# Gate and up of a decoder block in written order on all engines: three tiles ahead, staged work put on streams, reloads tied to progress, the up-side norm factor applied in the end

## The chip, the cores and the metric

The kernel runs on one core of a Trainium2 chip. The metric is the device time in microseconds (us) of one execution: the median of several runs of one program, where lower is better. Beside it stands one execution taken by the hardware profiler, which records every instruction of the engines: TensorE (PE, with its weight loads PEld), VectorE (DVE), ScalarE (ACT), GpSimd (POOL), and SyncE (SP), which only issues transfers. ScalarE and POOL issue transfers too.

## The reference

A decoder block of 256 tokens (16 meta tokens in front), width 2048: a projection into RWKV-7 time mixing and a forgetting attention, gated merge, output projection, then the feed-forward part. The change touches what stands behind the merge:

```python
merged = g_a * (y_a @ w_a) + g_b * (y_b @ w_b)
h = h + merged @ w_o                                          # (256, 2048)
gate, up = jnp.split(_rms(h, n2) @ w_gu, 2, axis=-1)          # w_gu: 2048 x 11264
return h + (jax.nn.silu(gate) * up) @ w_dn                    # w_dn: 5632 x 2048
```

`_rms` divides each token by the root of its mean square (the norm factor, one number per token) and multiplies by `n2`. Everything is float32. The matrix products run in fp32r on operands split into a high and a low part (`split`: ScalarE writes the high part as a copy in fp32r, VectorE the rest as a difference), as three products: high by high, low by high, high by low.

## The kernel before, in words

**Weights.** A weight tile is 128 partitions x 1024 elements, 0.5 MB. SP loads it into `raw`, ScalarE writes `wh` (L340), VectorE `wl` (L341), and TensorE multiplies by it. A job is a pair of functions, `load` and `mul`; `run` calls the load of one job before the `mul` of the job ahead of it. Outside the stages named below, a scheduler puts the instructions of each engine in an order by its own costs.

**Output projection.** Its tiles add to `hh` (the residual `h`, tokens on partitions), which is turned by TensorE, multiplied by `n2`, split into `hts` (features on partitions: the input of gate and up, not yet divided by the norm factor) and combined into sums of tokens, `hs0` to `hs7` (`sums_of_tokens`): each is split and written to DRAM by POOL (L1334).

**Gate and up.** The 5632 columns of each of gate and up are 11 groups of 512. Groups 0 to 7 (`PLAIN`) are multiplied plainly: eight tiles of gate, then eight of up per group (`gt`, `up`), the result with features on partitions, in four PSUM banks, the "main" ones. `halves` brings a bank to SBUF in two steps, a copy by ScalarE (L452) and an add by VectorE (L453). The gate's result is multiplied by the norm factor per token (`rsb`) and goes through Silu; the up's is multiplied by `rsb` (L1458) and by the gate (L1459), and split into `ach` and `acl`, the input of the down projection. For the groups of 256 features in `FAST`, sums of tokens `ss<i>` are built as above in one buffer (tag `hb`, `bufs=1`) and written to DRAM.

Groups 8 to 10 (`BLOCK`) are multiplied in 2 x 2 blocks with seven products in place of eight (a Strassen-Winograd scheme), in the four other, "aux", banks (`bg`, `bh`). A block tile `fr` has two halves: `load0` splits three of its four blocks into `fh` and `fl` (L515, L516) and forms four differences in place (L1492), `mul0` does three products; `load1` splits the differences into `wh`, `wl`, `mul1` does four products. The sums of tokens `hs` are the other operand: POOL reloads them from DRAM into `home` tiles (L1437). After the last tile of a block group, ScalarE and VectorE add the seven products up (`sums`, L1539), VectorE multiplies by the norm factor and by the gate (L1552), and a stream (`spawn`, called later by the planned clock that `slot` advances) turns the result by TensorE and splits it.

`todo` mixes the jobs: the block groups start at the places `STARTS`, and there one plain tile follows each half of a block tile. Only TensorE keeps the written order (`manual_schedule`); the order on the other engines is the scheduler's.

**Down projection.** Groups in `FAST` use the block scheme (`fast_jobs`: weights `q`, sums `sst` reloaded by POOL, products `dnp`), the others plain tiles (`slow_jobs`, products `dn`); both add to the main banks, and at the end of each half of the columns the banks are added to `hh`, reloaded from DRAM by POOL. All reloads of a half are issued ahead of its first tile (`sums_of`: L1598 for `sst`, L1600 for the fourth sum, which goes over an `ach` and `acl` block no longer needed).

## Time and profile before

| | |
|---|---|
| median of 3 runs | 1528.63 us (1527.79 to 1531.24) |
| profiled execution | 1529.84 us, its span 1528.1 us |
| granted TensorE clock, mean | 0.996 of full speed |
| TensorE busy | 1504.0 us of the span (98%) |
| weight loads, VectorE, ScalarE, POOL busy | 1343.3, 1241.2, 834.0, 134.9 us |
| moved | 306 MB, 201 GB/s over the span |

The span is the profiled execution from its first to its last record; its own time is 1.7 us longer. Gate and up take from about 788 to 1287 us, the down projection from there to the end. A row of instructions shows line, engine, operation, out<-in and shape, xcount, then busy time, mean duration in ns, and the idle time ahead of them with what ended most of it.

### The profile page before, as it was taken

Reading aid. Unit: us, or ns where it says so; the run is one execution under the profiler, and the core shown is the slowest. Engines: PE = TensorE matmul, PEld = TensorE weight load, DVE = VectorE, ACT = ScalarE, POOL = GpSimd, SP = SyncE. Lnnn points to the kernel's source line nnn. Section 1 sums busy time; section 2 is a strip of 40 time slices with the busy share of each in tenths; the row PEclk is TensorE's granted clock in tenths of the full one; section 3 lists DMA queues with packets and bytes.
Section 4 is the critical chain, followed back from the end, with each engine's and each line's share of the span. In section 5 each row is a group of like instructions: output and inputs, shape, how many; then the busy total and the mean of one; then the engine's idle time right before and its main releaser. Section 6 shows DMA issues by size and latency. Waiting matters only on the chain.

```text
span 1528.1 us, 26980 instructions
## 1 busy us (share of the span) xinstructions
PE 1504.0 (98%) x10320; PEld 1343.3 (88%) x10320; DVE 1241.2 (81%) x2180; ACT 834.0 (55%) x1212; POOL 134.9 (9%) x239
## 2 busy tenths in 40 slices
PE   9999999999999999999998999999999999899999
PEld 9999999999989888998887998998989888788887
DVE  7888699689789758776685888888898887698987
ACT  7754665465475546554454555555545555455553
POOL 2112202302202100000010000000000000200000
PEclk9999999999999999999999999999999999999999
DMA  8557356545645757767787666466775767966662
GB/s 270 166 173 203 116 157 196 168 125 169 186 125 161 222 139 231 237 215 252 255 276 240 195 214 200 148 198 218 216 224 182 223 184 209 377 224 205 223 214 84
DMA packets 217714, 306.45 MB, mean 201 GB/s; under 512 B 25136, under 2 KB 135232, under 8 KB 217456
## 3 DMA queue, kind: packets, MB, share of 16 engines
q1 hardware_dynamic: 202048, 277.25, 59.0%
q0 software_dynamic: 9488, 20.98, 4.0%
q10 hardware_dynamic: 6048, 6.49, 1.2%
q8 instruction: 81, 1.33, 0.4%
q14 instruction: 49, 0.40, 0.1%
HBM read 285.90 MB, written 18.78 MB: 199 GB/s over the span
## 4 chain that ended last, share of the span: by engine, by line
PE 83%; DVE 10%; issue 3%; DMA 2%; ACT 2%; SPq 0%; POOL 0%; DVEq 0%; ACTq 0%; POOLq 0%
PE zg L446 8%; PE up L446 5%; PE gt L446 5%; PE zg L448 4%; PE dn L1616 4%; PE dn L1614 4%; PE dn L1615 3%; DVE wl L341 3%; PE up L448 2%; PE gt L448 2%; PE f L446 2%; PE br L370 2%; PE br L371 2%; PE br L372 2%; PE f L370 2%
## 5 line engine op out<-in xcount | busy, mean ns | idle before, releaser
L341 DVE TENSOR_TENSOR wl<-raw,wh 128x1024 fp32r<-128x1024 f32 x402 | 489.7, 1225 | 112.3 <-ACT wh L340 110.2
L340 ACT ACTIVATE wh<-raw 128x1024 fp32r<-128x1024 f32 x402 | 421.7, 1055 | 256.7 <-PE br L371 40.6
L446 PE MATMUL gt<-hts,wh 128*128 128x512 f32 x512 | 181.0, 396 | 1.8 <-DVE ub L453 1.8
L446 PE MATMUL up<-hts,wh 128*128 128x512 f32 x512 | 180.0, 394 | 1.8 <-DVE gates L453 1.7
L446 PE MATMUL zg<-xhl,wh 128*128 128x512 f32 x512 | 181.2, 399 | 0.0
L448 PE MATMUL gt<-hts,wl 128*128 128x256 f32 x480 | 134.8, 281 | 0.0
L448 PE MATMUL up<-hts,wl 128*128 128x256 f32 x480 | 134.4, 280 | 0.0
L448 PE MATMUL zg<-xhl,wl 128*128 128x256 f32 x480 | 134.3, 280 | 0.0
L515 ACT ACTIVATE wh<-fr 128x1024 fp32r<-128x1024 f32 x48 | 50.9, 1061 | 115.6 <-DVE fr L1492 112.4
L446 PEld LDWEIGHTS gt<-hts,wh 128*128 128x128 f32 x512 | 95.0, 189 | 20.2 <-DVE ub L453 3.2
L446 PEld LDWEIGHTS up<-hts,wh 128*128 128x128 f32 x512 | 94.5, 188 | 19.8 <-DVE gates L453 2.7
L446 PEld LDWEIGHTS zg<-xhl,wh 128*128 128x128 f32 x512 | 94.3, 188 | 18.8 <-issue 0.7
L1614 PE MATMUL dn<-wh,ach 128*128 128x512 f32 x257 | 101.3, 394 | 1.0 <-ACT wh L515 1.0
L1615 PE MATMUL dn<-wh,acl 128*128 128x512 f32 x257 | 100.7, 392 | 0.0
L1616 PE MATMUL dn<-wl,ach 128*128 128x512 f32 x257 | 100.3, 394 | 0.1
L516 DVE TENSOR_TENSOR wl<-fr,wh 128x1024 fp32r<-128x1024 f32 x48 | 58.8, 1225 | 46.5 <-ACT wh L515 45.1
L448 PEld LDWEIGHTS gt<-hts,wl 128*128 128x128 f32 x480 | 91.2, 190 | 1.1
L448 PEld LDWEIGHTS zg<-xhl,wl 128*128 128x128 f32 x480 | 90.9, 189 | 1.2
L448 PEld LDWEIGHTS up<-hts,wl 128*128 128x128 f32 x480 | 90.9, 189 | 1.0
L1492 DVE TENSOR_TENSOR fr<-fr 128x256 f32<-128x256 f32 x192 | 80.9, 421 | 3.9
L515 ACT ACTIVATE wh<-tt 128x1024 fp32r<-128x1024 f32 x38 | 40.4, 1062 | 67.6 <-PE dn L1615 58.7
L370 PE MATMUL f<-xhl,wh 128*128 128x272 f32 x256 | 75.9, 296 | 0.0
(756 smaller groups left out, 3926.6 us busy)
## 6 DMA issues: line engine op xcount, KB each, us to landing
raw<-in_w_in_dram SPq DMA_DIRECT2D x160, 512.0 KB, 3.8
raw<-in_w_gate_up_dram SPq DMA_DIRECT2D x128, 512.0 KB, 4.5
raw<-in_w_down_dram SPq DMA_DIRECT2D x50, 512.0 KB, 4.7
fr<-in_w_gate_up_dram SPq DMA_DIRECT2D x48, 512.0 KB, 3.7
q<-in_w_down_dram SPq DMA_DIRECT2D x38, 512.0 KB, 5.8
raw<-in_w_o_dram SPq DMA_DIRECT2D x32, 512.0 KB, 5.0
raw<-in_w_branch_a_dram SPq DMA_DIRECT2D x16, 512.0 KB, 4.6
raw<-in_w_branch_b_dram SPq DMA_DIRECT2D x16, 512.0 KB, 4.0
```

Source lines behind the costliest of these rows:

```text
L340: nc.scalar.activation(th, rr, AF.Copy)
L341: nc.vector.tensor_tensor(tl, rr, th.bitcast(F32), op=ALU.subtract)
L370: nc.tensor.matmul(ps, wh, ah, start=first, stop=False)
L371: nc.tensor.matmul(ps, wh, al, start=False, stop=False)
L446: nc.tensor.matmul(ps.rearrange("p (a t) -> p a t", a=2), wh, act, start=first, stop=last)
L448: nc.tensor.matmul(ps[:, :T], wl, act[:, 0, :], start=False, stop=False)
L515: nc.scalar.activation(hi, src, AF.Copy)
L516: nc.vector.tensor_tensor(lo_, src, hi.bitcast(F32), op=ALU.subtract)
L1492: nc.vector.tensor_tensor(o, x_, y_, op=op)
L1614: nc.tensor.matmul(o, a[0], hi, start=first, stop=False)
L1615: nc.tensor.matmul(o, a[1], hi, start=False, stop=False)
L1616: nc.tensor.matmul(o, a[0], lo_, start=False, stop=last)
```

## The change

**Written order on all engines.** In gate and up, all five engines keep the order of the code. `run` is replaced by a loop that calls `load` for a job and the `mul` of the job three places (`AHEAD`) behind it, so that splits run three jobs ahead of the products, counted in halves of block tiles and plain tiles together.

**Staged work.** What follows a product's end is cut in two. The copies out of the banks stay at once; Silu, the gate's norm factor, the split of the result, and the sums of tokens become streams, called 2000 ns of planned clock later (`LATER`), the second sum another 2000 ns later. The transposes of a block result take both banks first, 6000 ns after its product with the gate (`FOLD`, 9000 before).

**Reloads tied to progress.** The `home` reloads leave one at a time as plain tiles are loaded, each behind `nudge`, a POOL copy of one column of the `wl` just split; it makes POOL wait for that split. In the down projection POOL keeps the written order too, and one group's `sums_of` and one eighth of `hh` leave per plain tile, behind a `nudge`.

**Which groups are fast.** `FAST` is 4 to 13 in place of 6 to 15, so the sums of tokens are built after the plain up groups 2 to 6 in place of 3 to 7.

**Norm factor in the end.** The up side is no longer multiplied by the norm factor, neither `ub` (L1458) nor `hb`; the adds of the down projection's banks to `hh` multiply by it (`scaled`).

**Layout.** A shift tile and tiles named ahead fix which buffers lie over which.

```diff
-FAST = list(range(6, 16))
+FAST = list(range(4, 14))
-FOLD = 9000
+FOLD = 6000
+AHEAD = 3
+LATER = 2000
...
-    for h_, d in zip(homes, hsd):
-        nc.gpsimd.dma_start(h_, d)
...
         def post_up(pss):
             ub = gu.tile([P, 4, T], F32, tag="ub", name=f"ub{j}")
             for m in range(4):
                 halves(ub[:, m], pss[m])
-            nc.vector.tensor_tensor(ub, ub, rb, op=ALU.mult)
             nc.vector.tensor_tensor(ub, ub, gs[0], op=ALU.mult)
-            split(*act_of(j), ub)
-            for i in range(2):
-                if 2 * j + i in FAST:
-                    ssd[2 * j + i] = sums_of_tokens(gu, "hb", 1, ...)
+            def rest():
+                split(*act_of(j), ub)
+                for i in range(2):
+                    if 2 * j + i in FAST:
+                        yield LATER
+                        ssd[2 * j + i] = sums_of_tokens(gu, "hb", 1, ...)
+            spawn(rest(), LATER)
...
             sums(hb, ps, f"bh{j}")
-            for t in range(2):
-                nc.vector.scalar_tensor_tensor(hb[:, t], hb[:, t], rs2[:, t:t + 1], gbs[0][:, t], op0=ALU.mult,
-                                               op1=ALU.mult)
             def turn():
+                nc.vector.tensor_tensor(hb, hb, gbs[0], op=ALU.mult)
+                yield FOLD
+                pts = [aux_ps(f"bt{j}{b}") for b in range(2)]
...
+    def nudge(w):
+        lo_ = w[0][1]
+        while len(lo_.shape) > 2:
+            lo_ = lo_[:, 0]
+        nc.gpsimd.tensor_copy(hp.tile([P, 1], F32, tag="nudge", name="nudge"), lo_[:, 0:1].bitcast(F32))
...
-    firm = tc.manual_schedule(engines={nc.tensor.engine})
+    firm = tc.manual_schedule(engines={e.engine for e in (nc.tensor, nc.vector, nc.scalar, nc.gpsimd, nc.sync)})
...
-    run(todo + plain[at:])
-    finish_job()
+    todo += plain[at:]
+    queue, loads = [], list(zip(homes, hsd))
+    for n, (load, mul) in enumerate(todo):
+        w = load()
+        queue.append((mul, w))
+        if len(queue) > AHEAD:
+            mul, v = queue.pop(0)
+            mul(v)
+        if loads and isinstance(w[0], tuple):
+            if n > 1:
+                nudge(w)
+            if n % 2 or n == 0 or n > STARTS[0]:
+                nc.gpsimd.dma_start(*loads.pop(0))
...
+    def scaled(t, o, x_):
+        nc.vector.scalar_tensor_tensor(o, x_, rs2[:, t:t + 1], o, op0=ALU.mult, op1=ALU.add)
...
-            nc.vector.tensor_tensor(hh[:, t, cs_], ps[:, c * n:(c + 1) * n], hh[:, t, cs_], op=ALU.add)
+            scaled(t, hh[:, t, cs_], ps[:, c * n:(c + 1) * n])
...
-    for i in QUICK[0]:
-        sums_of(i)
+    calm = tc.manual_schedule(engines={nc.gpsimd.engine})
+    calm.__enter__()
+    late = list(QUICK[0])
+    sums_of(late.pop(0))
+    pieces = [(t, slice(c * 512, (c + 1) * 512)) for c in range(4) for t in range(2)]
+
+    def then(load):
+        def f():
+            w = load()
+            nudge(w)
+            if late:
+                sums_of(late.pop(0))
+            if pieces:
+                t, cs_ = pieces.pop(0)
+                nc.gpsimd.dma_start(hh[:, t, cs_], hhd[:, t, cs_])
+            return w
+        return f
-            nc.gpsimd.dma_start(hh, hhd)
```

What this moves in the engines' queues is shown at three places. A row has the line, the operation, out<-in and the shape, with the number of the buffer behind a name.

The first place is POOL's queue at the end of the output projection, where the sums of tokens `hs` go to DRAM and come back as `home`. Before:

```order
L1334 DMA hs_9720<-hs4r 128x1024
L1334 DMA hs_9743<-hs5r 128x1024
L1437 DMA homeh_9969<-hs_9720 128x1024
L1437 DMA homel_9970<-hs_9743 128x1024
L1334 DMA hs_9914<-hs6r 128x1024
L1334 DMA hs_9937<-hs7r 128x1024
L1437 DMA homeh_9971<-hs_9914 128x1024
L1437 DMA home_9965<-hs_9318 128x1024
L1437 DMA home_9966<-hs_9341 128x1024
L1437 DMA home_9967<-hs_9519 128x1024
L1437 DMA home_9968<-hs_9542 128x1024
L1437 DMA homel_9972<-hs_9937 128x1024
```

And now:

```order
L1337 DMA hs_9915<-hs6r 128x1024
L1337 DMA hs_9938<-hs7r 128x1024
L1612 DMA home_9974<-hs_9319 128x1024
L1612 DMA home_9975<-hs_9342 128x1024
L1589 COPY nudge<-wl 128x1 x2
L1612 DMA home_9972<-hs_9520 128x1024
L1589 COPY nudge<-wl 128x1 x2
L1612 DMA home_9973<-hs_9543 128x1024
L1589 COPY nudge<-wl 128x1 x2
L1612 DMA homeh_9976<-hs_9721 128x1024
L1589 COPY nudge<-wl 128x1
L1612 DMA homel_9977<-hs_9744 128x1024
```

The first two reloads still stand right behind the writes of `hs6` and `hs7`; each later one stands behind one or two copies that wait for splits.

The second place is VectorE's queue after the end of the plain up group 3, where `ss6` and `ss7` are built among block tiles. Before, from the product with the gate on:

```order
L1459 TENSOR_TENSOR ub_12507<-ub_12507,gates_12172 128x1024
L1492 TENSOR_TENSOR fr<-fr 128x256
L1329 TENSOR_TENSOR ss6r<-ub_12507 128x128
L1331 TENSOR_TENSOR ss6r<-ub_12507 128x128
L1329 TENSOR_TENSOR ss6r<-ss6r,ub_12507 128x128
L1492 TENSOR_TENSOR fr<-fr 128x256
L516 TENSOR_TENSOR acl_12519<-ub_12507,ach_12518 128x1024
L1331 TENSOR_TENSOR ss6r<-ub_12507,ss6r 128x128
L1492 TENSOR_TENSOR fr<-fr 128x256 x2
L516 TENSOR_TENSOR ss6r<-ss6r 128x512
L516 TENSOR_TENSOR fl<-fr,fh 128x768
L516 TENSOR_TENSOR wl<-fr,wh 128x1024
```

And now, from the last add of the first sum on:

```order
L1334 TENSOR_TENSOR ss6r<-ub_12556,ss6r 128x128
L518 TENSOR_TENSOR ss6r<-ss6r 128x512
L518 TENSOR_TENSOR wl<-fr,wh 128x1024
L1332 TENSOR_TENSOR ss7r<-ub_12556 128x128
L1332 TENSOR_TENSOR ss7r<-ss7r,ub_12556 128x128
L1334 TENSOR_TENSOR ss7r<-ub_12556 128x128
L1334 TENSOR_TENSOR ss7r<-ub_12556,ss7r 128x128
L518 TENSOR_TENSOR ss7r<-ss7r 128x512
L343 TENSOR_TENSOR wl<-raw,wh 128x1024
L518 TENSOR_TENSOR fl<-fr,fh 128x768
L1505 TENSOR_TENSOR fr<-fr 128x256 x4
```

Before, three weight splits and two block differences stood between `ss6` and `ss7`; now a single block split does, and the sum of `ss7` stands ahead of the next plain tile's split.

The third place is VectorE's queue after the last tile of the block group `bh8`, whose seven products are added up. Before:

```order
L1539 TENSOR_TENSOR bh8bv<-bh_10879,bh8bu 128x256
L453 TENSOR_TENSOR gates_11539<-gates_11539,gt_0_11229 128x256
L1539 TENSOR_TENSOR hb_11504<-bh_10877,bh8bv 128x256
L1539 TENSOR_TENSOR bh8bu<-bh_10879,bh8bu 128x256
L1552 SCALAR_TENSOR_TENSOR hb_11504<-hb_11504,rs_9123,gates_10799 128x512
L1539 TENSOR_TENSOR hb_11504<-bh_10880,bh8bu 128x256
L1539 TENSOR_TENSOR hb_11504<-bh_10879,bh8bu 128x256
L453 TENSOR_TENSOR gates_11539<-gates_11539,gt_1_11230 128x256
```

And now, the last two of the seven sums and what follows them:

```order
L1552 TENSOR_TENSOR hb_11539<-bh_10912,bh8bu 128x256
L1552 TENSOR_TENSOR hb_11539<-bh_10911,bh8bu 128x256
L343 TENSOR_TENSOR wl<-raw,wh 128x1024
L1571 TENSOR_TENSOR hb_11539<-hb_11539,gates_10839 128x1024
L455 TENSOR_TENSOR gates_11573<-gates_11573,gt_0_11264 128x256
L455 TENSOR_TENSOR gates_11573<-gates_11573,gt_1_11265 128x256
L455 TENSOR_TENSOR gates_11573<-gates_11573,gt_2_11266 128x256
```

The adds that free the banks of the plain group (`gt_0` and so on) stood among the sums; now they stand behind all seven, a split and the product with the gate.

## The prediction

> **What bounds the kernel now.** I read the page first, then the granted clock by stretches, then TensorE's waits from the end of the output projection on, and last the queues at the places that these name.

> ```profile
> PE 1504.0 (98%) x10320; PEld 1343.3 (88%) x10320; DVE 1241.2 (81%) x2180; ACT 834.0 (55%) x1212; POOL 134.9 (9%) x239
> ...
> PEld bg L1504 <- ACT fh L515: 6.9, 1, 6.9
> PEld dnp L1614 <- issue: 3.4, 1, 3.4
> PEld gt L446 <- DVE ub L453: 3.2, 5, 1.7
> PEld up L446 <- DVE gates L453: 2.7, 3, 1.7
> PEld bg L1506 <- DVE wl L516: 2.0, 2, 1.6
> PEld bh L1506 <- DVE wl L516: 1.7, 3, 1.0
> PEld dn L1614 <- ACT wh L515: 1.3, 1, 1.3
> ...
> 810.00:815.00 5.00, 0.00 (x0) 0.00 (x0) 0.00 (x0) 0.26 (x1) 0.00 (x0) 0.86 1.10 395
> 815.00:820.00 5.00, 4.17 (x15) 3.58 (x16) 3.06 (x6) 2.07 (x3) 0.00 (x0) 0.50 0.34 127
> ...
> 1312.00:1316.00 4.00, 0.95 (x5) 0.51 (x3) 4.00 (x5) 1.57 (x2) 1.42 (x2) 0.93 1.27 401
> 1316.00:1320.00 4.00, 4.00 (x12) 3.21 (x13) 3.93 (x5) 2.87 (x4) 2.68 (x4) 0.65 1.25 407
> ```

> TensorE is the bound, so only its gaps can be won. In the waits (total, times, longest) the weight loads show seven rows of gaps in the stages touched, 21.2 us in all. The stretches (busy time of PE, PEld, DVE, ACT, POOL; granted clock; DMA share; GB/s) add that the clock fell to half after the two largest gaps. The first, A: 6.9 us idle, then about 4.8 us of matmuls at half clock (0.50 until 820), worth 2.4: 9.3 us. The second, B: 3.4 + 1.3 idle, then 4 x 0.35 / 0.5 = 2.8 us at half clock, worth 1.4: 6.1 us. The remaining 9.6 us (3.2 + 2.7 + 2.0 + 1.7) are short waits on VectorE, after which the clock stayed up.

> A and B are both queues of transfers:

> ```profile
> 799.86 2.20 POOL L1437 DMA_DIRECT2D home<-hs  x4
> 800.43 1.17 SPq L1486 DMA_DIRECT2D fr<-in_w_gate_up_dram  x2
> 814.74 0.84 ACT L515 ACTIVATE fh<-fr 128x768 fp32r<-128x768 f32 x1 [13.24 <-DMA fr<-in_w_gate_up_dram]
> ...
> 1303.57 0.29 DVE L1329 TENSOR_TENSOR ss15r<-ub 128x128 f32<-128x128 f32 x1 [2.88 <-DMA ss<-ss14r]
> 1305.34 0.69 DVE L516 TENSOR_TENSOR ss15r<-ss15r 128x512 fp32r<-128x512 f32 x1 [0.75 <-ACT ss15r L515]
> 1306.35 0.54 POOL L1334 DMA_DIRECT2D ss<-ss15r  x1 [1.14 <-DVE ss15r L516]
> 1306.88 3.53 POOL L1598 DMA_DIRECT2D sst<-ss  x5
> ```

> At 800 us the reloads of the token sums (home) share 395 GB/s with the first block tile (fr), which lands 14 us after its issue. At 1305 us the reloads for the down projection (sst) stand in POOL's queue behind the write of ss15, and that behind VectorE, which waited for ss14 to leave the one buffer.

> **The change part by part.** *Reloads tied to progress (A).* The home reloads now leave one every one or two weight tiles, behind a small POOL copy that waits for that tile's split; fr stands in SP's queue behind seven tiles and before the eighth, not behind eleven. The burst is gone, and VectorE asks for fr only after the split of tile 6. Gain 9.3; bounds 0 (fr still late) and 9.3. I take 9.3, since the 3 MB of that burst spread over some 30 us is 100 GB/s beside the tiles. The copies cost POOL alone, which is 9% busy; a split tile is held until its copy ran, four tiles later at the earliest.

> *FAST 4 to 13, sums_of per slow tile (B).* The sums of 12 and 13 are written before the last plain block, so that nothing stands before the first sst in POOL's queue at the end of gate and up, about 20 us before it is read. Its 8 pieces of hh and 9 sst come one set per slow tile. Gain 6.1; bounds 0 and 6.1; I take 6.1 (the q reload moves up in SP's queue as well, from behind twelve tiles to behind eight).

> *Up-side factor at the end.* This removes eight VectorE products with rsb, and in the down projection makes the adds scaled ones.

> ```profile
> L1458 DVE TENSOR_TENSOR ub<-ub,rsb 128x1024 f32<-128x1024 f32 x8 | 9.7, 1217 | 0.0
> L516 DVE TENSOR_TENSOR wl<-fr,wh 128x1024 fp32r<-128x1024 f32 x48 | 58.8, 1225 | 46.5 <-ACT wh L515 45.1 <-PE gt L446 1.2
> L1552 DVE SCALAR_TENSOR_TENSOR hb<-hb,rs,gates 128x512 f32<-128x512 f32 x6 | 4.4, 740 | 0.0
> 1409.78 0.68 DVE hh L1715
> ```

> 9.7 us of VectorE go, which is no path time by itself. A scaled add at 0.74 against 0.68 costs 0.06, a few of which stand at the end: nothing.

> *Program order on all engines, three tiles ahead.* TensorE's own matmuls stay the same in number and order but for the transposes of the block outputs. A plain tile is now split between a block tile's differences (fr) and its second split, which fills the idle 45.1 us of L516. SP issues in the same order: an fr waits for the second split two block tiles back, with the later tiles behind it, but six splits (over 7 us) lie between that and its own use, against 3.7 to land: nothing. ScalarE keeps the order of VectorE. But what follows a product's end now stands in a fixed place of VectorE's queue, with every later split behind it.

> ```profile
> 1063.43 0.28 PE L1504 MATMUL bh<-fh,hts 128*128 128x256 f32 x1
> 1071.48 0.28 PE L1504 MATMUL bh<-fh,hts 128*128 128x256 f32 x1
> ...
> 1067.81 0.95 DVE L516 TENSOR_TENSOR fl<-fr,fh 128x768 fp32r<-128x768 f32 x1
> 1068.68 1.22 DVE L341 TENSOR_TENSOR wl<-raw,wh 128x1024 fp32r<-128x1024 f32 x1
> 1069.82 1.80 DVE L1492 TENSOR_TENSOR fr<-fr 128x256 f32<-128x256 f32 x4
> ...
> fr<-in_w_gate_up_dram SPq DMA_DIRECT2D x48, 512.0 KB, 3.7
> ...
> 1281.83 1.06 ACT L340 ACTIVATE wh<-raw 128x1024 fp32r<-128x1024 f32 x1 [1.71 <-PE up L446]
> 1284.60 1.06 ACT L340 ACTIVATE wh<-raw 128x1024 fp32r<-128x1024 f32 x1 [1.71 <-PE up L446]
> 1286.84 1.50 DVE L453 TENSOR_TENSOR ub<-ub,up 128x256 f32<-128x256 f32 x4
> 1288.37 1.23 DVE L1458 TENSOR_TENSOR ub<-ub,rsb 128x1024 f32<-128x1024 f32 x1
> ...
> 1057.39 0.54 POOL L1334 DMA_DIRECT2D ss<-ss6r  x1 [254.14 <-DVE ss6r L516]
> 1060.90 0.54 POOL L1600 DMA_DIRECT2D ach<-ss  x1 [2.97 <-DMA ss<-ss6r]
> 1064.30 0.54 POOL L1334 DMA_DIRECT2D ss<-ss7r  x1 [2.33 <-DVE ss7r L516]
> 1070.52 0.54 POOL L1600 DMA_DIRECT2D ach<-ss  x1 [5.68 <-DMA ss<-ss7r]
> 1185.42 0.55 POOL L1334 DMA_DIRECT2D ss<-ss10r  x1 [56.56 <-DVE ss10r L516]
> 1188.59 0.54 POOL L1600 DMA_DIRECT2D ach<-ss  x1 [2.63 <-DMA ss<-ss10r]
> ```

> TensorE takes 1284.60 - 1281.83 = 2.77 us for a plain tile and 1071.48 - 1063.43 = 8.05 for two plain tiles with both halves of a block tile, so 2.51 for these, by their three and four products 1.08 and 1.43.

> Take the end of up 3 as zero, when the splits of the next three tiles are done. VectorE has the halves at 1.0 (up 7 ended a tile after 1284.60, at 1287.4, and L1458 began at 1288.37) and the gate product at 2.2. Then in its new order, each step from one start to the next: split of the plain tile four ahead 1.14 (3.35), fl and four differences 0.87 + 1.75 (5.97), acl 1.14 (7.1), a split (8.25), the first sum 2.46 from first add to end, as for ss15 (10.7). The block split behind it waits for ScalarE, which had the sum first (12.25). The second sum needs the one buffer: the first one's write leaves at 8.25 + 2.78 = 11.05 (1303.57 to 1306.35 for ss15) and lands 3.3 later (3.51 for ss6, 3.17 for ss10), at 14.35. Its adds and ScalarE's part end at 16.1; only then does ScalarE split the plain tile eight ahead, to 17.15, and VectorE, to 18.4. TensorE comes to that tile at 1.08 + 2.77 + 1.43 + 2.77 + 1.08 + 2.77 + 1.43 = 13.3, or 13.6 as the block split at 12.25 is late too, and reads VectorE's part 0.2 later: 4.6 lost, with that 0.3 4.9. At ups 2 and 4 the block tile stands one place later, and the same count gives 4.6; up 5 is as up 3; up 6 lies among plain tiles alone, where the lead suffices. Sum 2 x 4.9 + 2 x 4.6 = 19.0. Ends: 2.4 each if the write cost nothing (9.6), 7.7 each if it lands in 6.2 like ss7 (30.8). I take 3.3, the nearest rows: both are first sums among block tiles.

> *Bank waits.* After the last block tile of bh8 and bh10, VectorE's queue holds a split, seven sums, a split and the product hb before the halves of the plain tile that ends 2.77 later, and TensorE goes straight on to a tile in the same banks. Before, the scheduler put sums and halves in turns. Two sums stand in one row:

> ```profile
> 952.99 0.74 DVE L1539 TENSOR_TENSOR hb<-bh,bh8bu 128x256 f32<-128x256 f32 x2
> ```

> With 0.36 for one of them, the first bank is free at 0.9 + 2.5 + 1.15 + 1.15 + 0.35 = 6.05 after the block's end, and is wanted at 2.77: 3.3 lost, twice: 6.6. Ends: 4.4 (as now, the longest of the 3.2 and 2.7 above) and 8. I take the count.

> The short waits of the first table (9.6) are inside these counts or gone: gain 9.6, of which 1.2 at ups 0 and 1, which have no sums.

> *The clock.* Six gaps of 3.3 to 4.8 us. The gap of 3.0 to 3.4 at 1312 us was followed by 2.8 us at half clock, the short ones of 1.7 by none. I take 1.0 us lost for each, 6.0; ends 0 and 1.7 each (10.2). [...]

> **The sum.** -9.3 - 6.1 - 9.6 + 19.0 + 6.6 + 6.0 = +6.6. The profiled execution took 1529.84 (span 1528.1), 1.2 above the median of the runs shown, 1528.63. Against that execution: 1536.4; beside the median: 1535.2. I round to 1535. A difference of 0.2%, 3.1 us, is about what a measurement of this kernel can tell from none.

> **The rivals.** *Faster: the sums do not hold VectorE up.* If at the four places the second sum finds its buffer free and its splits in time, they cost what the short waits cost now, 9.6 - 4.4 = 5.2 together: -25.0 + 5.2 + 6.6 + 2.0 (the clock at two gaps) = -11.2, 1517, or 1513 with the bank waits as now. The other terms make -16.4, so this decides from (16.4 - 3.1) / 4 = 3.3 us per place downward, its clock included; from 3.3 to 4.9 no difference can be told. For it speaks that VectorE loses 45 us of idle time and 9.7 of work; against it, that both sums stand ahead of the eighth tile, and that ss15 did wait for ss14's write.

> *Slower still: the writes land like ss7's*, in 6.2 us: 4 x 2.9 more, 1547.

> *The reloads stay in the way.* POOL's first two leave without waiting, right behind hs6 and hs7. If fr or q is late for them or for others, A or B stays: 1541 to 1544. Against it: two at once, not six, and sst stands first in its queue.

> **How the numbers follow.** Forecast case (1532 to 1540, its own range) 0.36; slow writes 0.08; reloads still late 0.06; no difference 0.18; faster 0.32, as a queue order can hide more than a count shows. Slower: 0.36 + 0.08 + 0.06 = 0.50. The range goes from 1514, which leaves out the last part of the faster case, to 1547, the slow writes.

> **What would show it.** A right: no PE wait on fh near 815 us, and clock 1.00 there. B right: sst issued before 1295 us, no gap at 1312. The order right or wrong: waits of VectorE on the writes of ss4, ss6, ss8, ss10 and TensorE gaps of 4 to 5 us some 14 us after the ends of ups 2 to 5, with half clock behind them. If those gaps are below 3 us, or the second sum waits for nothing, the forecast is wrong and the time is under 1527.

## The result, and the profile after

The changed kernel took 1548.96 us (median of 4 runs, 1548.26 to 1551.02) against 1528.75 for the kernel before on the same chips: a ratio of 1.0132, 95% interval 1.0114 to 1.0149. It is slower, the way that was forecast, but by 20 us and not by 7. The profiled execution took 1548.26 us, with a span of 1546.5, 18.4 longer than before; the sums below are made against the two spans.

First the waits of the weight loads from the output projection's end on, as before (us in total, times, longest):

```profile
PEld gt L448 <- ACT wh L342: 14.2, 4, 3.7
PEld gt L450 <- DVE wl L343: 4.1, 4, 1.1
PEld up L448 <- DVE gates L455: 3.9, 1, 3.9
PEld gt L448 <- DVE ub L455: 3.9, 1, 3.9
PEld up L450 <- DVE wl L343: 3.1, 4, 0.8
PEld bh L1519 <- DVE wl L518: 1.1, 2, 0.9
PEld dn L1653 <- DVE wl L343: 0.8, 1, 0.8
PEld dn L1651 <- DVE hh L1739: 0.6, 2, 0.4
```

The waits on `fh` and `dnp` (6.9, 3.4 and 1.3 us before) are gone; there are six new large ones: four on a split of a gate tile (3.4 to 3.7 and then up to 1.1), two on a bank (3.9 each). The total is 31.7 us. Before, it was 23.3: the seven rows that the prediction shows, 21.2, and five smaller ones, 2.1 (0.2 us at `hT` stand in both and are left out):

```profile
PEld dn L1616 <- DVE wl L341: 0.6, 1, 0.6
PEld bg L1506 <- DVE fl L516: 0.5, 1, 0.5
PEld dnp L1616 <- DVE wl L516: 0.4, 1, 0.4
PEld dnp L1614 <- ACT wh L515: 0.3, 1, 0.3
PEld bh L1504 <- ACT wh L515: 0.3, 1, 0.3
```

Next the places of the old gaps and the six stretches at half clock (from:to, length, busy time of PE, PEld, DVE, ACT, POOL, granted clock, DMA share, GB/s):

```profile
800.00:820.00 20.00, 20.00 (x126) 18.01 (x125) 15.65 (x27) 10.21 (x13) 6.81 (x11) 1.00 1.04 369
...
1300.00:1320.00 20.00, 20.00 (x104) 17.05 (x103) 12.27 (x13) 10.43 (x13) 7.73 (x14) 1.00 0.78 230
...
943.95:950.78 6.83, 5.57 (x17) 4.80 (x18) 5.91 (x11) 0.75 (x1) 0.00 (x0) 0.50 0.26 77
995.15:998.56 3.41, 3.18 (x10) 2.79 (x11) 3.38 (x5) 2.50 (x3) 0.00 (x0) 0.50 0.63 195
1063.41:1070.24 6.83, 5.33 (x15) 4.24 (x16) 6.32 (x9) 4.45 (x6) 0.53 (x1) 0.50 0.65 229
1135.10:1138.51 3.41, 3.41 (x12) 2.88 (x11) 3.34 (x5) 1.96 (x3) 0.00 (x0) 0.50 0.71 222
1203.36:1210.19 6.83, 5.68 (x17) 4.49 (x18) 6.39 (x9) 4.33 (x5) 0.53 (x1) 0.50 0.59 199
1261.39:1268.22 6.83, 5.19 (x16) 4.42 (x17) 6.16 (x9) 1.06 (x1) 0.00 (x0) 0.50 0.39 94
...
sum 34.14, PE 28.35 PEld 23.62 DVE 31.49 ACT 15.05 POOL 1.07; mean PE 4.73 PEld 3.94 DVE 5.25 ACT 2.51 POOL 0.18
```

```profile
813.64:820.47 6.83, 4.64 (x17) 4.05 (x18) 3.53 (x6) 2.81 (x4) 0.00 (x0) 0.50 0.46 170
1315.40:1318.81 3.41, 2.94 (x7) 2.39 (x8) 3.34 (x4) 2.84 (x3) 2.37 (x4) 0.50 1.29 405
```

That is 7.58 us at half clock, 3.8 lost. So waits +8.4 and clock +10.4: 18.8, where the span grew by 18.4. The 0.4 between them is not explained.

One of the four split places, the end of up 3, in VectorE's, POOL's and ScalarE's own times (start, duration, idle time ahead with its releaser):

```profile
1061.71 0.29 DVE L1332 TENSOR_TENSOR ss7r<-ub 128x128 f32<-128x128 f32 x1 [1.95 <-DMA ss<-ss6r]
...
1064.42 1.23 DVE L343 TENSOR_TENSOR wl<-raw,wh 128x1024 fp32r<-128x1024 f32 x1 [0.26 <-ACT wh L342]
...
1058.57 0.53 POOL L1337 DMA_DIRECT2D ss<-ss6r  x1 [63.88 <-DVE ss6r L518]
...
1062.81 0.63 ACT L517 ACTIVATE ss7r<-ss7r 128x512 fp32r<-128x512 f32 x1 [4.31 <-DVE ss7r L1334]
1063.35 1.04 ACT L342 ACTIVATE wh<-raw 128x1024 fp32r<-128x1024 f32 x1
```

The second sum waits 1.95 us for the write of `ss6` to leave the one buffer (issued at 1058.57, let go at 1061.71: 3.1 us), and the split of the plain tile stands behind it: the chain that the prediction counted. It runs through two queues: ScalarE stands 4.31 us idle for the second sum, with the plain tile's `wh` behind it, and it is this `wh` that TensorE waits for.

And the first bank place, at the end of bh8:

```profile
939.57 0.42 DVE L1552 TENSOR_TENSOR hb<-bh,bh8bu 128x256 f32<-128x256 f32 x1
...
942.48 1.22 DVE L343 TENSOR_TENSOR wl<-raw,wh 128x1024 fp32r<-128x1024 f32 x1
943.61 1.22 DVE L1571 TENSOR_TENSOR hb<-hb,gates 128x1024 f32<-128x1024 f32 x1
944.74 1.41 DVE L455 TENSOR_TENSOR gates<-gates,gt 128x256 f32<-128x256 f32 x4
```

ScalarE had copied the four banks by 942.1, but the adds that free them stand behind sums, split and product until 944.74.

### The profile page after: what moved, and what is told of

It is laid out like the page before. It is cut to its first block, busy times and chain, and to the rows that moved or that the text cites. A ratio compares the mean times of both kernels' runs of the same rounds, so it can differ in the third digit from the quotient of the medians.

```text
span 1546.5 us, 26976 instructions
## 1 busy us (share of the span) xinstructions
PE 1513.6 (98%) x10320; PEld 1351.3 (87%) x10320; DVE 1248.5 (81%) x2169; ACT 838.8 (54%) x1212; POOL 147.5 (10%) x263
## 4 chain that ended last, share of the span: by engine, by line
PE 71%; issue 25%; DVE 3%; ACT 1%; DMA 1%; POOL 0%; SPq 0%; DVEq 0%; POOLq 0%; ACTq 0%
PE zg L448 8%; PE dn L1653 4%; PE dn L1651 4%; PE dn L1652 4%; PE zg L450 4%; PE gt L448 3%; PE f L448 2%; PE br L372 2%; PE br L373 2%; PE br L374 2%; PE f L372 2%; PE wo L1361 2%; PE wo L1363 2%; PE wo L1362 2%; PE up L448 2%
## 5 line engine op out<-in xcount | busy, mean ns | idle before, releaser
L342 ACT ACTIVATE wh<-raw 128x1024 fp32r<-128x1024 f32 x402 | 423.3, 1056 | 256.1 <-PE wo L1362 37.9
L448 PE MATMUL gt<-hts,wh 128*128 128x512 f32 x512 | 189.7, 411 | 16.9 <-ACT wh L342 13.4
L448 PE MATMUL up<-hts,wh 128*128 128x512 f32 x512 | 182.3, 398 | 3.6 <-DVE gates L455 3.6
L448 PE MATMUL zg<-xhl,wh 128*128 128x512 f32 x512 | 181.1, 399 | 0.0
L450 PE MATMUL gt<-hts,wl 128*128 128x256 f32 x480 | 139.4, 290 | 2.5 <-DVE wl L343 2.5
L448 PEld LDWEIGHTS gt<-hts,wh 128*128 128x128 f32 x512 | 99.3, 197 | 36.5 <-ACT wh L342 14.2
L448 PEld LDWEIGHTS up<-hts,wh 128*128 128x128 f32 x512 | 95.7, 190 | 21.3 <-DVE gates L455 3.9
L448 PEld LDWEIGHTS zg<-xhl,wh 128*128 128x128 f32 x512 | 94.3, 188 | 18.7 <-issue 0.7
L1651 PE MATMUL dn<-wh,ach 128*128 128x512 f32 x257 | 101.2, 394 | 0.0
L450 PEld LDWEIGHTS gt<-hts,wl 128*128 128x128 f32 x480 | 95.7, 199 | 5.1 <-DVE wl L343 4.1
L374 PE MATMUL f<-xhl,wl 128*128 128x272 f32 x256 | 73.6, 288 | 0.0
## 6 DMA issues: line engine op xcount, KB each, us to landing
raw<-in_w_in_dram SPq DMA_DIRECT2D x160, 512.0 KB, 3.9
raw<-in_w_gate_up_dram SPq DMA_DIRECT2D x128, 512.0 KB, 4.8
raw<-in_w_down_dram SPq DMA_DIRECT2D x50, 512.0 KB, 4.7
fr<-in_w_gate_up_dram SPq DMA_DIRECT2D x48, 512.0 KB, 3.8
q<-in_w_down_dram SPq DMA_DIRECT2D x38, 512.0 KB, 6.2
raw<-in_w_o_dram SPq DMA_DIRECT2D x32, 512.0 KB, 4.8
raw<-in_w_branch_a_dram SPq DMA_DIRECT2D x16, 512.0 KB, 4.1
raw<-in_w_branch_b_dram SPq DMA_DIRECT2D x16, 512.0 KB, 3.3
```

The costliest lines, as they stand in the source:

```text
L342: nc.scalar.activation(th, rr, AF.Copy)
L374: nc.tensor.matmul(ps, wl, ah, start=False, stop=last)
L448: nc.tensor.matmul(ps.rearrange("p (a t) -> p a t", a=2), wh, act, start=first, stop=last)
L450: nc.tensor.matmul(ps[:, :T], wl, act[:, 0, :], start=False, stop=False)
L1651: nc.tensor.matmul(o, a[0], hi, start=first, stop=False)
```

## The experiments

All runs are of one core, with a profile, and timed in 3 rounds beside the kernel before on the same chip; its median there was 1530.1 to 1530.6 us, so the ratios compare better than the medians do. The theory from the trace, Q: the written order, of VectorE's queue above all, makes the six gaps, and with them the 3.41 or 6.83 us at half clock behind each. The rivals stand in each expectation.

### The buffer alone

```diff
-sums_of_tokens(gu, "hb", 1, f"ss{2 * j + i}", ...)
+sums_of_tokens(*((acp, f"l{BLOCK[-1]}") if i else (gu, "hb")), 1, f"ss{2 * j + i}", ...)
```

> The changed kernel (1548.3 us profiled), with the second sum of tokens of each plain up group in a buffer of its own; the order on every engine stays. Theory Q (queue order): at the four places the buffer wait is only 1.0, 1.95, 1.0 and 1.95 us of VectorE's idle time before the second sum, so the gaps of 4.8 to 5.7 us shrink by that alone: 5.9 us less idle, at most 4 us less half clock where a gap falls below 3 us: 1538 to 1542. Theory B (the buffer): the gap at each place is the write's 3.5 us landing, as the prediction priced it (4.7 to 2.4 each): 9 us less idle and the clock restored (6.9 us): 1532 or below. Theory N: the buffer is not what ends the wait: 1548.

Measured: 1539.81 us, ratio 1.0057 (1.0040 to 1.0074).

```profile
PEld gt L448 <- ACT wh L342: 7.6, 4, 2.5
PEld gt L450 <- DVE wl L343: 4.2, 4, 1.1
```

The time lies in Q's range. The waits on `wh` fall from 14.2 to 7.6 and no further: the wait for the buffer is a part, the place of the two sums in the queue the larger one. Theory B falls. Half clock stays as well: 0.50 from 1127.59 to 1134.42 us at the end of up 4, and a granted clock of 0.991 over the span against 0.988 in the changed kernel.

### The second sum later

```diff
-                        yield LATER
+                        yield LATER if i == 0 else 10000
```

> The changed kernel with the second sum of tokens called 10000 ns of planned clock after the first in place of 2000, in the same one buffer. Theory Q (both sums stand ahead of the tile that is late): the four gaps with their half clock, 6.2 to 7.7 us each and 27.2 in all, go: 1521 to 1525. Rival L (VectorE has too little slack among block tiles, wherever the sums stand): each place keeps a gap of at least 2 us somewhere later: 1535 to 1545.

Measured: 1526.59 us, ratio 0.9972 (0.9959 to 0.9985): 24 us less than the changed kernel by the ratios, and faster than the kernel before. The row `gt L448 <- ACT wh L342` is gone from the waits. What is left at the four places are waits of up to 1.0 us, 0.7 to 1.9 in all at each, which the expectation left out, so the time is 1.6 us above Q's range; the clock stays at 1.00 there (0.997 over the span, the two bank places included, against 0.988 in the changed kernel). It is Q, with a small part of L.

### The adds of the block products later

```diff
-            sums(hb, ps, f"bh{j}")
 
             def turn():
+                sums(hb, ps, f"bh{j}")
                 nc.vector.tensor_tensor(hb, hb, gbs[0], op=ALU.mult)
...
-            spawn(turn(), LATER)
+            spawn(turn(), 3000)
```

> The changed kernel with the adds of the seven products of bh8 to bh10 (and the product with the gate behind them) called 3000 ns of planned clock after the block's end, so that they stand behind the copies out of the plain group's banks. Theory Q: the two gaps at 941 and 1263 us (3.7 and 3.7 us longest, 6.9 and 6.7 with small ones and half clock) go: 1534 to 1537. Rival A: the aux banks come free later, and the next block group, four plain tiles on, waits for them: at least 3 us of new gaps at bg9's start: 1538 or more.

Measured: 1545.72 us, ratio 1.0099 (1.0083 to 1.0114).

```profile
PEld bg L1517 <- issue: 5.0, 2, 3.1
...
959.87 0.36 PE L1517 MATMUL bg<-wh,home 128*128 128x256 f32 x1 [2.84 <-DVE acl L518]
```

The two bank rows of 3.9 us are gone, so the sums ahead of the copies are shown as their cause. But bg9 and bg10 wait instead (5.0 us). For the weight load the profile names only "issue"; the row of the product behind it names VectorE's split of the turned block result (`acl`), which reads the transposes out of two aux banks: it starts at 959.04 us, 0.8 ahead of that product, where the changed kernel has 5.2 (955.80 and 960.95). Rival A takes two thirds of the gain that Q expected.

### Both edits

> The two edits together: second sum 10000 ns later, and the adds of bh8 to bh10 behind the plain copies. Theory Q: all six gaps go, 27.2 + 13.6 = 40.8 us: 1507 to 1512. If the places depend on each other (a gap taken away moves a later one up): above 1515.

Measured: 1523.76 us, ratio 0.9952 (0.9938 to 0.9967), only 3 us better than the second sum alone, and the two intervals overlap: the waits of bg9 and bg10 on the aux banks stay (5.0 us in 2), and the one of bg9 is followed by 6.8 us at half clock (959.4 to 966.2). The places depend on each other.

### Only the gate product behind the copies

With the late second sum:

```diff
-            spawn(turn(), LATER)
+            spawn(turn(), 3000)
```

> The kernel with the late second sum (1526.6 us), with only the product of a block result with the gate called 3000 ns after the block's end in place of 2000, so that it stands behind the copies out of the plain group's banks; the seven adds stay ahead of them. [...] Rival: another engine frees the banks, no change: 1526.5.

By Q the product's 1.15 us goes from each of the two bank waits, for a time of 1521 to 1525 us.

Measured: 1525.34 us, ratio 0.9959 (0.9944 to 0.9974). Both bank waits go from 3.9 to 2.8 us, by the product's 1.15; behind the first the clock is still 0.50 (944.11 to 947.52 us), behind the second it is 1.00 (1244.40 to 1247.80). New waits of bg9 and bg10 (3.8 us in 2) take most of it back: the time is 0.3 us above Q's range, and its interval overlaps with that of the late second sum alone.

### Block groups one tile later

With the late second sum:

```diff
-STARTS = (7, 24, 43, 60, 79, 96)
+STARTS = (7, 25, 43, 60, 79, 97)
-FOLD = 6000
+FOLD = 3000
```

> The kernel with the late second sum (1526.6 us), with the block groups bh8 and bh10 begun one plain tile later (25 and 97 in place of 24 and 96), so that the plain group's banks are copied out before the block's products are added up, and the transposes of a block result called 3000 ns after its gate product in place of 6000. Theory Q: the two places of 5.9 us each go: 1513 to 1517. Rival A (as the moved adds showed): three tiles are too few for sums, transposes and splits before the next block group takes the four aux banks, and bg9 waits 3 us or more: 1518 or more. [...]

Measured: 1529.19 us, ratio 0.9994 (0.9985 to 1.0004). Not the gain of Q:

```profile
PEld bt L402 <- DVE hb L1571: 6.6, 3, 3.5
PEld up L448 <- DVE gates L455: 2.9, 2, 2.7
PEld gt L448 <- DVE ub L455: 2.7, 1, 2.7
```

The transposes, called 3000 ns after their product in place of 6000, now wait for it (6.6), and bank waits of 2.7 us come up at 878 and 1174 us, where with the later start no half of a block tile stands any more between the last tile of a plain group and the first of the next. Neither of the two is followed by half clock; the granted clock over the span is 0.998. Rival A had the sign right and the place wrong; the two edits of this run were not tried one by one.

### VectorE and ScalarE to the scheduler

```diff
-    firm = tc.manual_schedule(engines={e.engine for e in (nc.tensor, nc.vector, nc.scalar, nc.gpsimd, nc.sync)})
+    firm = tc.manual_schedule(engines={e.engine for e in (nc.tensor, nc.gpsimd)})
```

> The changed kernel with the written order kept on TensorE and POOL alone; VectorE, ScalarE and SyncE are ordered by the scheduler again, as in the kernel before. Theory Q (the order of the queues makes the six gaps): they shrink to what such places cost before, 9.6 us in all, and the two large ones of before stay gone: 1513 to 1519. Rival S (the staged streams and the sums themselves cost it): 1535 or more.

Measured: 1522.92 us, ratio 0.9955 (0.9941 to 0.9970): 27 us less than the changed kernel. Rival S falls, since the streams, the sums, the buffer and the spread of the reloads are the same. The expected 1513 to 1519 was missed by one place, where TensorE waits 5.0 us for the first block tile:

```profile
799.45 1.50 SPq L1499 DMA_DIRECT2D fr<-in_w_gate_up_dram  x2
...
813.10 0.84 ACT L517 ACTIVATE fh<-fr 128x768 fp32r<-128x768 f32 x1 [11.35 <-DMA fr<-in_w_gate_up_dram]
```

With SyncE in the scheduler's order the first `fr` leaves at 799.45, behind two of the reloads (798.59). In the changed kernel it left ahead of them all:

```profile
790.54 0.37 SPq L1499 DMA_DIRECT2D fr<-in_w_gate_up_dram  x1
...
798.60 0.83 ACT L517 ACTIVATE fh<-fr 128x768 fp32r<-128x768 f32 x1
```

So SyncE was put back, with VectorE and ScalarE left to the scheduler (`engines` of tensor, gpsimd and sync):

> The changed kernel with the written order on TensorE, POOL and SyncE; VectorE and ScalarE are ordered by the scheduler. With SyncE left to the scheduler too the time was 1522.9 us, of which 4.9 us idle and 3.6 us behind it at 809 to 823 us, because the first block tile left at 799 us with the reloads; in the written order it left at 790.5 us. Theory Q: that place costs at most 1.1 us again, the rest stays as it was: 1514 to 1517. Rival: the scheduler's order on VectorE does not fit the written order of the loads, and tiles are late elsewhere: 1520 or more.

Measured: 1516.74 us, ratio 0.9907 (0.9889 to 0.9925): in Q's range, the fastest version, and faster than both kernels. Its largest waits:

```profile
PEld up L448 <- DVE gates L455: 5.7, 7, 1.5
PEld bh L1517 <- ACT wh L517: 2.3, 2, 1.5
```

None is over 1.5 us, and its granted clock is 1.000 over the span. That VectorE and ScalarE were freed together leaves open which of the two queues the gain needs; the chain above runs through both.

### The home reloads alone, in the kernel before

```diff
-    for h_, d in zip(homes, hsd):
-        nc.gpsimd.dma_start(h_, d)
...
-    firm = tc.manual_schedule(engines={nc.tensor.engine})
+    firm = tc.manual_schedule(engines={e.engine for e in (nc.tensor, nc.gpsimd)})
...
-    run(todo + plain[at:])
+    run([(then(load), mul) for load, mul in todo + plain[at:]])   # then: the POOL copy and one reload, as in the change
```

With the spread goes the written order on POOL, which keeps each copy ahead of its reload.

> The kernel before, with the home reloads alone spread: one at once, then one every one or two plain tiles behind a POOL copy. The prediction's term A: the gap at 808 us with its half clock goes, 9.3 us: 1519 to 1521. Rival: the first block tile is late anyway, or the reloads are late for the first block product: 1524 or more.

Measured: 1523.66 us, ratio 0.9959 (0.9944 to 0.9974), so 6.3 us less, and a span of 1520.2, 7.9 below that of the kernel before: between what was expected and the rival. The wait on `fh` and its half clock are gone, with 1.0 us of a short one left between 800 and 806 us. Another 1.5 us are lost at B, not at A: the gap there is now followed by 6.83 us at half clock (5.97 us of work in them, from 1305.23 to 1312.06) in place of 3.41 (2.94). Term A is real and its size about right. But the first `fr` also left earlier, at 797.28 in place of 800.43 us, 1.1 ahead of the first reload (798.39), so this run does not show that the spread alone does it.

### The choice of fast groups alone, in the kernel before

```diff
-FAST = list(range(6, 16))
+FAST = list(range(4, 14))
```

> The kernel before, with the fast groups 4 to 13 in place of 6 to 15 and nothing else. The prediction's term B: the gap at 1309 to 1319 us goes (6.2 us), a new short wait at the end of up 2 of 0 to 2 us: 1522 to 1526. Rival: the reloads for the down projection, still all at once, hold up the weight tiles at its start: no gain, 1528 to 1531.

Measured: 1528.80 us, ratio 0.9995 (0.9986 to 1.0005).

```profile
PEld dnp L1616 <- DVE wl L516: 1.7, 1, 1.7
PEld gt L448 <- DVE wl L341: 1.5, 1, 1.5
PEld bg L1504 <- ACT wh L515: 1.3, 1, 1.3
```

The gap at 1309 us and its half clock are gone, as term B said, and the wait on `fh` fell to 5.4, but 1.7 us wait at the start of the down projection instead, with sums of tokens at up 2 too there are new waits of 1.3 and 1.5 us behind ups 2 and 3, and at 953 us there is a new stretch at half clock. Taken by itself, the part is worth nothing.

### The norm factor back on the up side

With the late second sum; the adds of the down projection are plain again:

```diff
+            nc.vector.tensor_tensor(ub, ub, rb, op=ALU.mult)
             nc.vector.tensor_tensor(ub, ub, gs[0], op=ALU.mult)
...
-                nc.vector.tensor_tensor(hb, hb, gbs[0], op=ALU.mult)
+                for t in range(2):
+                    nc.vector.scalar_tensor_tensor(hb[:, t], hb[:, t], rs2[:, t:t + 1], gbs[0][:, t], ...)
...
-        nc.vector.scalar_tensor_tensor(o, x_, rs2[:, t:t + 1], o, op0=ALU.mult, op1=ALU.add)
+        nc.vector.tensor_tensor(o, x_, o, op=ALU.add)
```

> The kernel with the late second sum (1526.6 us), with the norm factor back on the up side (eight products with rsb of 1.22 us, bh's product in two of 0.74 us) and plain adds in the down projection. The prediction's term: VectorE's 9.7 us are no path time, the sum of it nothing: 1525 to 1528, the 1.0 us gap at the end of the first half of the columns a few tenths smaller. Rival V (with the written order each microsecond in VectorE's queue behind an up group's end is late splits): 1.2 us at each of the six up groups among block tiles and 0.3 at the two bank places, 7.8 in all: 1532 to 1537.

Measured: 1533.20 us, ratio 1.0018 (1.0008 to 1.0027): 7 us above the same kernel without it. Rival V holds:

```profile
PEld gt L450 <- DVE wl L343: 10.6, 12, 1.7
```

The same row has 5.3 us in 6 with the late second sum alone: each up group's end has a longer queue, and there are twice as many waits on the splits behind it.

### Two tiles ahead

With the late second sum:

```diff
-AHEAD = 3
+AHEAD = 2
```

> The kernel with the late second sum (1526.6 us), with splits two jobs ahead in place of three. Theory Q (the lead of the splits is all that hides the staged work): the lead is shorter by one job, 1.1 to 2.8 us, at each of the 16 ends of plain groups and the sums: 15 us or more slower, 1540 or above, with new half-clock windows. Rival: the lead does not matter, buffers do: 1525 to 1529.

Measured: 1543.11 us, ratio 1.0077 (1.0061 to 1.0093), 16 us above three ahead: the lead of the splits is what hides the staged work.

## Why the prediction was wrong, point by point

**A and B: right.** Both gaps went, and `fr` was in time. For A the prediction gave two reasons, the spread of the reloads and the earlier place of `fr` in SyncE's queue. With the spread and `fr` leaving at 799.45 us, behind two reloads, 5.0 of the 6.9 us stayed; where it left at 797.28, ahead of them, the wait went. So the spread does not suffice, and the place of `fr` counts; the place without the spread was not run. B's gap went as said, and the choice of fast groups alone takes it away, though it gains no time by itself.

**The split places: right in mechanism, place and size.** The prediction had 4.9 and 4.6 us at the ends of ups 2 to 5, 19.0 in all; the profile has 14.2 + 4.1 + 1.1 = 19.4, 4.6 to 5.3 each, and the prediction's own chain (sum, write, second sum, split) is visible row by row. Where the prediction put its lower end, 2.4 each with no wait for the write, the buffer of its own left 7.6 + 4.2 + 0.8 = 12.6 us, 3.2 each. The rival that the sums do not hold VectorE up is refuted.

**The bank waits: right, a little small.** 3.9 us each against 3.3: seven sums, a split and the product took 5.17 us, from 939.57 to 944.74, where the count had 4.8. 1.2 us of the miss.

**"The short waits are inside these counts or gone": wrong.** 3.1 us on `wl` of up tiles and 0.8 + 0.6 in the down projection stay, 4.5 us that the sum had at nothing. The first come from the gates: VectorE's product with `rsb` and ScalarE's Silu behind it now stand ahead of the next tile's split, three times; the fourth, at 1033 us, stands behind the sums and Silu of bg9. The scaled adds of the down projection, costed at nothing, bring at most the 0.6 of `dn L1651 <- DVE hh L1739`.

**"I take 1.0 us lost for each": wrong, and the largest term.** The six gaps cost 14.2 us of clock where the prediction had 6.0, 2.4 each. It had read the price of a gap from one case, and its end of 1.7 us was no bound: four of the six were followed by 6.83 us at half clock. 8.2 us of the miss.

**"No path time by itself" for the 9.7 us of the norm factor: wrong** as a statement, though the count of the split places had already left these products out, so no term of the sum rests on it. In the written order, with the late second sum, it is worth 7 us.

The terms miss by 1.2 + 4.5 + 8.2 and 0.4 of the split places, 14.3. The five short rows of before that the sum left out, 2.1, go the other way: 12.2, where the span is 11.8 above the forecast (18.4 less 6.6). The range ended at 1547, the slow writes with every other term as taken. Joined with the clock's own upper end, 4.2 us more, it would have held the time, but by luck: the writes were not slow (3.1 us at up 3), and the clock cost more than that end.

## What to carry to other kernels

In these runs the written order on VectorE and ScalarE made every wait in their queues a wait of all that stood behind. Keep such an order for the engines that only need a sequence (the matmuls, the issuing of transfers), and let work that follows a product's end sit where the next splits have a lead, or leave the engines that carry both to the scheduler. Here the written order on TensorE, POOL and SyncE, with VectorE and ScalarE free, was 34 us better than on all five. Price a gap of TensorE with its clock: in the changed kernel 3.41 us at half clock cost 1.7 us where TensorE worked all through them (from 1135.10) and 1.4 on average (14.2 us lost in 34.14), and places whose longest waits were 3.4 to 3.9 us had 3.41 or 6.83 us of it behind them.

## What the runs showed of the hardware

The six stretches at half clock of the changed kernel are 3.41 or 6.83 us long, and TensorE was not idle all through the time ahead of them: it worked 1.10 us in the 3.41 us ahead of the first and 0.81 in the 3.39 ahead of the one at 1135.10 us (after the length stands PE's busy time, and the clock after POOL's):

```profile
940.54:943.95 3.41, 1.10 (x7) 0.69 (x5) 3.33 (x7) 1.63 (x4) 0.00 (x0) 1.00 0.55 165
943.95:947.37 3.42, 2.16 (x7) 1.87 (x8) 3.38 (x7) 0.00 (x0) 0.00 (x0) 0.50 0.52 153
947.37:950.78 3.41, 3.41 (x12) 2.92 (x12) 2.52 (x5) 0.75 (x1) 0.00 (x0) 0.50 0.00 0
950.78:954.19 3.41, 3.41 (x21) 2.98 (x21) 2.12 (x2) 2.84 (x4) 0.00 (x0) 1.00 0.00 0
...
1128.30:1131.71 3.41, 1.73 (x13) 1.44 (x12) 2.25 (x8) 0.00 (x0) 0.00 (x0) 1.00 0.39 159
1131.71:1135.10 3.39, 0.81 (x3) 0.50 (x4) 2.39 (x4) 3.20 (x4) 0.53 (x1) 1.00 0.06 25
```

And two of the kernel before with the other fast groups alone, then one of the kernel with the block groups one tile later:

```profile
949.77:953.18 3.41, 1.67 (x9) 0.95 (x7) 3.41 (x10) 1.72 (x3) 0.00 (x0) 1.00 0.85 288
953.18:956.60 3.42, 3.38 (x11) 2.89 (x12) 3.42 (x7) 0.60 (x1) 0.00 (x0) 0.51 0.17 65
...
878.43:881.84 3.41, 1.60 (x9) 1.42 (x10) 3.41 (x7) 1.44 (x3) 0.00 (x0) 1.00 0.00 0
```

The 1.67 us of work at 950 us were followed by half clock too (0.51). Full clock followed the 1.73 us at 1128 us, 1.97 at 1241 us in the kernel with the gate product moved, and the 1.60 at 878 us. So in these rows the column of PE's busy time does not tell which came next: 1.67 us had half clock behind them and 1.60 full clock.

Nor did the length of a wait give its price. The two bank waits of the changed kernel, 3.9 us each, had 6.83 us at half clock behind them (943.95 and 1261.39 us). Of its four split places the two whose longest wait was 3.7 us had 3.41 (995.15 and 1135.10), and the two with 3.4 had 6.83 (1063.41 and 1203.36).
